# A hybrid decoder block on one core: two output blocks fed in turn, gates and compression inputs reordered, one norm factor and one load moved to ScalarE

## The chip, the cores and the metric

The kernel runs on 1 core of one Trainium2 chip. The metric is the device time of one execution in microseconds (us), as the median of several runs. Five engines work side by side, each through its own queue in program order: PE (TensorE, matrix products into PSUM), DVE (VectorE), ACT (ScalarE), POOL (GpSimd) and SP (SyncE, which here only issues DMA transfers). They wait for one another through semaphores. The profile's PEld is PE's loading of the stationary operand, which overlaps its products.

## What is computed

One decoder block over 512 tokens and a model width of 2048, all in fp32:

```python
hn   = rmsnorm(x, norm1_g)
proj = hn @ w_in                      # q_a k_a v_a | q_b | k_c v_c | k_s v_s | k_w v_w | g_b
# mixer A, 8 heads: windows (128,1) (512,4) (2048,16) of (window, dilation), mixed by their
# softmax denominators, ALiBi slopes
o_a  = dilated_mixture(q_a, k_a, v_a)
# mixer B, 8 heads in 2 key/value groups: keys and values compressed over blocks of 32
# (stride 16) by silu(flat(block + pe) @ w1) @ w2; selected blocks; sliding window
kc, vc = compress_blocks(k_c, ...), compress_blocks(v_c, ...)
g    = sigmoid(g_b)                   # three gates for each head and token
o_b  = g0 * compressed(q_b, kc, vc) + g1 * selected(q_b, k_s, v_s) + g2 * window(q_b, k_w, v_w)
h    = x + concat(rmsnorm(o_a, grp_norm_a), rmsnorm(o_b, grp_norm_b)) @ w_out
hn2  = rmsnorm(h, norm2_g)
h    = h + (silu(hn2 @ w_gate) * (hn2 @ w_up)) @ w_down      # hidden width 5632
out  = rmsnorm(h, final_g)
```

## The kernel before

**Layout and precision.** Features lie on the 128 partitions, the 512 tokens on the free axis. Every fp32 product is made of three products in a reduced format: an operand X is split into a high part h (ACT, a copy that rounds) and a low part l (DVE, X minus h), and PE adds `wh*ah + wh*al + wl*ah` (`mm3`, lines 164 to 167; `mm`, lines 1009 to 1012). `ah` and `al` hold the split activations, 16 blocks of 128 features each.

**The weight stream.** `plan()` lists the units of weights (128 x 1024) in the order in which they are used; SP loads them four ahead into `raw` (`load_to`, line 102). Each unit is two *halves* of 128 x 512, and each half is a `Job`: `first()` is the ACT copy to `wh` (line 136), `second()` the DVE subtraction to `wl` (line 139). `wh` and `wl` have five buffers, so a half's copy can start once PE has used up the half five before it. `next_half()` (line 172) hands PE the next half; at that place in the program the `first()` of the half three further on is emitted and the `second()` of the half two further on, then what `later(n, f)` has put off by n halves. `run_unit` (line 193) runs the products of a list, four blocks of 128 x 128 to a half, and calls `side_hook` after every second block: in it, the small tasks of a stage are slipped between PE's products.

**The stages.**

1. Input blocks (lines 278 to 308): SP loads `sm` (all small constants and gains, 64 KB), then the blocks `xc` of x and the weights. `split_act` (line 252) multiplies a block by its gain from `sm` while it splits it into `ah`, `al`. PE makes the four compression inputs `pc` (k_c and v_c of two groups) as the blocks arrive, then the 24 gate columns `pg` (lines 315 to 317). The factor 1/rms is made for tokens by `Rsqrt`, and `Spread` (line 230) turns it into a full 128 x 512 tile: four 128 x 128 diagonal matrices (identity times a column, line 237, DVE), then four products with ones (line 243). The result is `r1`.
2. Shared keys and values of group 0 (`kv_group`, line 658): the projections ks, kw, vs, vw, two half-units each of 24 products. Meanwhile eight `kv_part` tasks (line 330), one for each side hook, scale `pc` by `r1` into `kv_src` (line 333, DVE, for every second task), add the position embedding in another order of elements (line 341, DVE: it reads `kv_src` with a step of 16 elements and writes `ku` in sequence), and split the result (line 343, ACT; line 328, DVE). After the first half-unit of ks, `gates_out` scales `pg` (line 360, DVE), transposes it on PE (line 363) and makes the gates. The first layer of the compression, 16 units `w1` (line 370) of eight short products (256 columns), is laid between the projections as `W1_AFTER` says: for each name, how many units follow its two half-units. The w1 units use the `kv_part` results; after unit 7 and unit 15 ACT copies the sums to `hids` (line 386), and `compressed(s)` (line 388) does the rest in two steps.
3. Heads (lines 694 to 726): for each of 8 j, projections qb, qa, ka, va, with attention in the side hook: `step()` (line 581) alternates between scores (`s_steps`) and transposes with the product by values (`t_steps`, the last of them `pv`). A `pv` step waits at least `SLACK` = 2 steps after the last transposes. In the last head, after the first half of va, `split_act` for the eight blocks of mixer B (into `ah[0..7]`) is put off over the next four halves, two blocks to a half.
4. Output projection (lines 886 to 896): 16 blocks of 128 features over the B half, then 16 over the A half. Each block (`out_unit`, line 830) has a PSUM bank (tag `proj` for blocks 0 and 1; there are two `proj` banks, and the last va projection has used one of them, which `evac_v`, line 441, reads out on DVE), two halves of weights, and needs `ah[0..3]` in its first half, `ah[4..7]` in its second. `last_steps` finishes the attention here; when it is idle, `close_attention` splits the A blocks, makes the group norms and loads x again.
5. FFN: for each of 44 blocks f of hidden features, seven products P1 to P7 of 256 columns (a Strassen-like scheme; `product`, line 997), then combinations on DVE (`after`, line 1027); a down projection after each four f. For f = 0 the norm factors are made on the way (lines 1089 to 1097): two `Spread`s, `inv` and `r2`. P1's PSUM bank is read at line 1047 before f = 1 can start in it.
6. The last down projection and the final norm (`last`, line 1104).

## Time and profile before

| | |
|---|---|
| median of 3 runs | 2183.11 us (2182.37 to 2186.63) |
| the profiled execution's own time | 2182.41 us |
| its span, first to last instruction | 2180.6 us |
| PE busy | 2161.7 us (99%), 15776 products |
| DVE busy | 1568.4 us (72%) |
| ACT busy | 970.5 us (45%) |
| granted TensorE clock | 0.998 |
| moved by DMA | 232.28 MB, mean 107 GB/s |

The profile page gives busy time by engine, the chain of work that ended last, and groups of instructions by source line. The lists of waits name, for each engine, the instruction that waited and what it waited for. The timeline gives every instruction with its start and length; PE's products are pipelined, so that the pace of PE is read from start to start (a product of 512 columns takes a row of about 0.39 us, while the next starts about 0.23 us after it). What stands in square brackets at the end of a timeline row is the time the engine sat idle before it, and what released it. Two instructions of one kind that follow each other are merged in one row, with their count behind an x.

### The profile page before, as it was taken

The page shows a single profiled execution, that of the slowest core. Times are in us where ns is not written, and L with a number is a line of the kernel's source. Part 1 is how long each engine was busy: PE and PEld are TensorE (multiplying, and loading weights), DVE is VectorE, ACT ScalarE, POOL GpSimd, SP SyncE. Part 2 cuts the span into 40 slices and gives each one's busy share as a digit, 9 for nine tenths or more (in the row PEclk, how much of TensorE's full clock was granted, in tenths as well). Part 3 has the DMA queues.
Part 4 walks back from the last instruction along what each step waited for, and adds up shares of the span by engine and source line. Part 5 has one row for each costly group of instructions (what it writes and reads, how often), then busy time and mean ns, then how long its engine had stood idle before and what let it go on. Part 6 is the DMA issues. An engine that isn't in the chain of part 4 may idle for free.

```text
span 2180.6 us, 39719 instructions
## 1 busy us (share of the span) xinstructions
PE 2161.7 (99%) x15776; PEld 2021.7 (93%) x15776; DVE 1568.4 (72%) x3046; ACT 970.5 (45%) x1862; POOL 43.7 (2%) x51
## 2 busy tenths in 40 slices
PE   9999999999999999999999999999999999999997
PEld 7788888888887889999999999999999999999997
DVE  6755666356667578979687786869596877868686
ACT  6544444244444255535344443535353444435356
POOL 0000000000000000000000000000000000000003
PEclk9999999999999999999999999999999999999999
DMA  6442222322134334343333333333333333333233
GB/s 223 145 138 80 80 81 68 99 90 80 58 100 154 97 97 107 117 117 93 107 112 108 96 117 102 112 88 117 117 98 107 108 112 93 117 107 108 80 125 107
DMA packets 81866, 232.28 MB, mean 107 GB/s; under 512 B 8848, under 2 KB 11536, under 8 KB 81680
## 3 DMA queue, kind: packets, MB, share of 16 engines
q1 hardware_dynamic: 80960, 228.17, 33.2%
q0 software_dynamic: 720, 1.57, 0.5%
q8 instruction: 124, 2.03, 0.4%
q14 instruction: 62, 0.51, 0.1%
HBM read 225.51 MB, written 4.19 MB: 105 GB/s over the span
## 4 chain that ended last, share of the span: by engine, by line
PE 96%; DVE 2%; ACT 1%; issue 0%; DMA 0%; SPq 0%; DVEq 0%; ACTq 0%
PE P L1012 15%; PE P L1010 15%; PE P L1011 15%; PE pp L165 6%; PE pp L167 6%; PE pp L166 6%; PE pd L1011 4%; PE pd L1010 4%; PE pd L1012 4%; PE pab L166 3%; PE pab L167 3%; PE pab L165 3%; PE pt L515 1%; PE psc L167 1%; PE psc L166 1%; PE psc L165 1%
## 5 line engine op out<-in xcount | busy, mean ns | idle before, releaser
L136 ACT ACTIVATE wh<-raw 128x512 fp32r<-128x512 f32 x888 | 549.2, 628 | 533.5 <-PE P L1011 209.6
L139 DVE TENSOR_TENSOR wl<-raw,wh 128x512 fp32r<-128x512 f32 x888 | 596.5, 685 | 47.4 <-ACT wh L136 46.9
L1012 PE MATMUL P<-ah,wl 128*128 128x256 f32 x1552 | 428.9, 276 | 0.3 <-DVE wl L139 0.3
L1010 PE MATMUL P<-ah,wh 128*128 128x256 f32 x1552 | 428.8, 276 | 0.0
L1011 PE MATMUL P<-al,wh 128*128 128x256 f32 x1552 | 428.8, 276 | 0.0
L1012 PEld LDWEIGHTS P<-ah,wl 128*128 128x128 f32 x1552 | 291.4, 188 | 0.5 <-DVE wl L139 0.5
L1011 PEld LDWEIGHTS P<-al,wh 128*128 128x128 f32 x1552 | 291.4, 188 | 0.0
L1010 PEld LDWEIGHTS P<-ah,wh 128*128 128x128 f32 x1552 | 291.4, 188 | 0.0
L165 PE MATMUL pp<-ah,wh 128*128 128x512 f32 x640 | 260.5, 407 | 0.0
L167 PE MATMUL pp<-ah,wl 128*128 128x512 f32 x640 | 251.0, 392 | 0.0
L166 PE MATMUL pp<-al,wh 128*128 128x512 f32 x640 | 250.3, 391 | 0.0
L754 DVE TENSOR_TENSOR raw<-raw 128x512 f32<-128x512 f32 x346 | 237.3, 686 | 3.4
L1010 PE MATMUL pd<-ah,wh 128*128 128x256 f32 x784 | 216.6, 276 | 0.0
L1012 PE MATMUL pd<-ah,wl 128*128 128x256 f32 x784 | 216.6, 276 | 0.0
L1011 PE MATMUL pd<-al,wh 128*128 128x256 f32 x784 | 216.5, 276 | 0.0
L136 ACT ACTIVATE wh<-rawd 128x512 fp32r<-128x512 f32 x160 | 101.2, 632 | 247.8 <-PE pd L1011 123.5
L1078 DVE TENSOR_TENSOR hs<-hs,pd 128x512 f32<-128x512 f32 x98 | 67.4, 688 | 122.9 <-PE pd L1012 122.7
L1011 PEld LDWEIGHTS pd<-al,wh 128*128 128x128 f32 x784 | 147.2, 188 | 0.0
L1010 PEld LDWEIGHTS pd<-ah,wh 128*128 128x128 f32 x784 | 147.2, 188 | 0.0
L1012 PEld LDWEIGHTS pd<-ah,wl 128*128 128x128 f32 x784 | 147.2, 188 | 0.0
L167 PEld LDWEIGHTS pp<-ah,wl 128*128 128x128 f32 x640 | 120.2, 188 | 27.9
L139 DVE TENSOR_TENSOR wl<-rawd,wh 128x512 fp32r<-128x512 f32 x160 | 110.1, 688 | 40.7 <-ACT wh L136 35.6
(275 smaller groups left out, 4565.4 us busy)
## 6 DMA issues: line engine op xcount, KB each, us to landing
raw<-in_wst_dram SPq DMA_DIRECT2D x310, 512.0 KB, 3.5
rawd<-in_wdn_dram SPq DMA_DIRECT2D x160, 256.0 KB, 2.6
bias<-in_bias_dram SPq DMA_DIRECT2D x16, 320.0 KB, 3.0
xc<-in_xt_dram SPq DMA_DIRECT2D x16, 256.0 KB, 3.3
hs<-in_xt_dram SPq DMA_DIRECT2D x16, 256.0 KB, 5.0
fin<-in_wdn_dram SPq DMA_DIRECT2D x8, 512.0 KB, 3.9
out_dram<-hs SPq DMA_DIRECT2D x8, 256.0 KB, 2.1
out_dram<-scaled SPq DMA_DIRECT2D x3, 512.0 KB, 2.8
```

What stands on the lines that cost most here:

```text
L136: act.activation(self.h, self.src(), AF.Copy)
L139: dve.tensor_tensor(self.l, self.src(), self.h.bitcast(F32), op=OP.subtract)
L165: pe.matmul(o, wh, mh, start=start, stop=False)
L166: pe.matmul(o, wh, ml, start=False, stop=False)
L167: pe.matmul(o, wl, mh, start=False, stop=stop)
L515: pe.transpose(p[:, 128 * (o + b):128 * (o + b) + 128], self.e[t][:, 128 * b:128 * b + 128], ident)
L754: return lambda: dve.tensor_tensor(o(), o(), x(), op=OP.add)
L1010: pe.matmul(o, wh, mh, start=start, stop=False, skip_group_check=True)
L1011: pe.matmul(o, wh, ml, start=False, stop=False, skip_group_check=True)
L1012: pe.matmul(o, wl, mh, start=False, stop=stop, skip_group_check=True)
L1078: dve.tensor_tensor(hs[:, nb, :], hs[:, nb, :], p, op=OP.add)
```

## The change

- `W1_AFTER`: after the change the 16 w1 units follow the projections in groups of 3 (after kw's second half-unit), 4 and 3 (vs), 3 and 3 (vw); before, in groups of 3 and 3 (kw), 3 and 3 (vs), 2 and 2 (vw).
- Output projection: the weight halves of blocks 0 and 1 are used in turn (block 0 first half, block 1 first half, block 0 second half, block 1 second half), and both `proj` banks are taken at the start.
- `Spread` can make its diagonals on ACT; the factor `inv` before the FFN does so.
- `sm` is loaded by a DMA that ACT issues and not SP.
- `kv_part`: the scaling writes `kv_src` in the element order that the addition reads, with a step of 32 elements; the addition reads it in sequence.
- The scaling of `pg` becomes a task of its own, third in the list of tasks, ahead of the third `kv_part`.
- `step()`: for the last head, the `pv` steps wait one step more (`late`).
- In `after` for f = 0 the reading of P1's bank comes one DVE instruction earlier.

```diff
-W1_AFTER = {"ks": (0, 0), "kw": (3, 3), "vs": (3, 3), "vw": (2, 2)}
+W1_AFTER = {"ks": (0, 0), "kw": (0, 3), "vs": (4, 3), "vw": (3, 3)}
...
     n_plain = len(jobs)
+    k = 2 * units.index(("out", 0, 1))
+    jobs[k + 1], jobs[k + 2] = jobs[k + 2], jobs[k + 1]
...
-        def __init__(self, col):
+        def __init__(self, col, on_act=False):
...
             for t in range(self.n):
-                dve.tensor_scalar(self.r[:, 128 * t:128 * t + 128], ident, col[:, t:t + 1], None, op0=OP.mult)
+                r = self.r[:, 128 * t:128 * t + 128]
+                if on_act:
+                    act.activation(r, ident, AF.Copy, scale=col[:, t:t + 1])
+                else:
+                    dve.tensor_scalar(r, ident, col[:, t:t + 1], None, op0=OP.mult)
...
-    sp.dma_start(sm, smalls)
+    act.dma_start(sm, smalls)
...
             kv_src[0] = tmp()
-            dve.tensor_tensor(kv_src[0], pc[2 * s + g], r1, op=OP.mult)
-        tv = kv_src[0].rearrange("p (c i) -> p i c", i=16)
+            dve.tensor_tensor(kv_src[0].rearrange("p (i c) -> p c i", i=16),
+                              pc[2 * s + g].rearrange("p (c i) -> p c i", i=16),
+                              r1.rearrange("p (c i) -> p c i", i=16), op=OP.mult)
+        tv = kv_src[0].rearrange("p (i c) -> p i c", i=16)
...
+    gated = []
+
+    def gates_in():
+        gated.append(tmp())
+        dve.tensor_tensor(gated[0][:48, :], pg[:48, :], r1[:48, :], op=OP.mult)
+
+    tasks.insert(2, gates_in)
+
     def gates_out():
-        t = tmp()
-        dve.tensor_tensor(t[:48, :], pg[:48, :], r1[:48, :], op=OP.mult)
+        t = gated[0]
...
-    cur = {"s": None, "t": None, "ready": deque(), "turn": 0}
+    cur = {"s": None, "t": None, "ready": deque(), "turn": 0, "late": 0}
...
-                    if is_pv and (cur["tat"] + SLACK > now[0] or (a.v is not None and not a.v.ready())):
+                    if is_pv and (cur["tat"] + SLACK + cur["late"] > now[0] or (a.v is not None and not a.v.ready())):
...
             if j == NH - 1 and half == 0:
+                cur["late"] = 1
...
-    for nb in range(KB):
+    first = [ps.tile([128, 512], F32, tag="proj", name="pab", bufs=2) for _ in range(2)]
+    run_unit([(first[n], ah[:, 4 * k + s, :], al[:, 4 * k + s, :], k == 0 and s == 0, k == 1 and s == 3)
+              for k in range(2) for n in range(2) for s in range(4)])
+    pab.extend(enumerate(first))
+    for nb in range(2, KB):
...
         elif name == "P6":
             sub(g[:, HI], g[:, LO], x("P6"))
+            if not f:
+                dve.tensor_tensor(g[:, LO], x("P1"), st["r2"][:, LO], op=OP.mult)
             add(u[:, LO], g[:, HI], x("P7"))
             if not f:
-                dve.tensor_tensor(g[:, LO], x("P1"), st["r2"][:, LO], op=OP.mult)
...
-                later(1, lambda r=r: st.update(inv=Spread(r.z), r2=Spread(r.y)))
+                later(1, lambda r=r: st.update(inv=Spread(r.z, True), r2=Spread(r.y)))
```

## The prediction, written before the result was known

> **What bounds the kernel now.** I read the page first, then the list of PE's waits, then the timeline round each wait.
>
> ```profile
> PE 2161.7 (99%) x15776; PEld 2021.7 (93%) x15776; DVE 1568.4 (72%) x3046; ACT 970.5 (45%) x1862; POOL 43.7 (2%) x51
> PE 96%; DVE 2%; ACT 1%; issue 0%; DMA 0%; SPq 0%; DVEq 0%; ACTq 0%
> ```
>
> PE is busy for 99% of the span and holds 96% of the chain that ended last. The change takes no product away from PE, so all it can win is time in which PE waits. These waits are few, and each has a place:
>
> ```profile
> PE pab L166 <- DVE al L255: 1.6, 2, 0.9
> PE phid L383 <- DVE wl L139: 1.6, 2, 1.1
> PE pgt L363 <- ACT kvs L343: 1.3, 1, 1.3
> PE po L165 <- ACT et_h L523: 0.4, 1, 0.4
> ...
> PE pc L166 <- DVE al L255: 0.3, 1, 0.3
> ```
>
> Columns: us in total, times, longest; the two rows left out, 0.3 each, stand in the FFN's part below. These rows count from the modelled end of the product before. Start to start, a wait costs more: the next product should start 0.23 us after one of 512 columns (64.74 and 64.97 below), 0.12 us after one of 256 (24 of them from 88.82 to 91.55 below), and the first after a wait is slow by another 0.1 us. So I take each loss from starts. All of this makes some 9 us out of 2180: the change cannot win more than about 0.4%.
>
> **The start.**
>
> ```profile
> 0.74 0.38 SPq L278 DMA_DIRECT2D sm<-in_smalls_dram  x1
> 1.18 0.42 SPq L283 DMA_DIRECT2D xc<-in_xt_dram  x1
> sm<-in_smalls_dram SPq DMA_DIRECT2D x1, 64.0 KB, 1.8
> 2.03 0.20 ACT L93 ACTIVATE ident<-ones 128x1 f32<-128x1 f32 x1
> 6.92 0.63 ACT L136 ACTIVATE wh<-raw 128x512 fp32r<-128x512 f32 x1 [1.28 <-DMA raw<-in_wst_dram]
> ```
>
> Without `sm` in front, every load on SP is issued 0.44 us earlier (1.18 - 0.74). ACT's second weight copy waits for its load until 6.92; the next blocks of x follow behind that copy on ACT, and PE's wait for `al` behind them. So the gain is up to 0.44 us, if `sm` is there in time. On ACT it is issued at 0.74 at the earliest, at 2.23 (2.03 + 0.20) at the latest, and took 1.8 us on SP: it lands between 2.5 and 4.0. No row shows a DMA issued by ACT. At the worst I let `sm` land with the slowest load, at 6.92: then the split of x and the first weight copy (0.63 each) come before the second copy, and 1.3 us are lost. I take a gain of 0.35, near the issue rows. A landing up to about 5.6 costs nothing.
>
> [...]
>
> **Gates and compression.**
>
> ```profile
> 64.74 0.39 PE L166 MATMUL pp<-al,wh 128*128 128x512 f32 x1
> 64.97 0.39 PE L167 MATMUL pp<-ah,wl 128*128 128x512 f32 x1
> 66.63 0.42 PE L363 MATMUL pgt<-ident,tmp 48*128 48x48 f32 x4 [1.27 <-ACT kvs L343]
> L341 DVE TENSOR_TENSOR ku<-tmp,sm x8: 1014/1028/1053, 59.4 to 75.1; 128x512 f32<-128x512 f32 x4, 128x496 f32<-128x496 f32 x4
> L333 DVE TENSOR_TENSOR tmp<-pc,r x4: 683/690/701, 58.7 to 72.7; 128x512 f32<-128x512 f32 x4
> 77.99 0.28 PE L382 MATMUL phid<-wh,kvs 128*128 128x256 f32 x1
> 83.23 0.28 PE L383 MATMUL phid<-wl,kvs 128*64 128x256 f32 x1
> 88.82 0.28 PE L382 MATMUL phid<-wh,kvs 128*128 128x256 f32 x1
> 91.55 0.28 PE L383 MATMUL phid<-wl,kvs 128*64 128x256 f32 x1
> 79.79 4.29 DVE L139 TENSOR_TENSOR wl<-raw,wh 128x512 fp32r<-128x512 f32 x7
> 99.25 0.39 ACT L386 ACTIVATE osb<-phid 128x256 f32<-128x256 f32 x1 [0.33 <-PE phid L383]
> 108.75 0.28 PE L382 MATMUL phid<-wh,kvs 128*128 128x256 f32 x1
> 109.11 0.34 PE L383 MATMUL phid<-wl,kvs 128*64 128x256 f32 x1
> ```
>
> The transposes of the gates start at 66.63 and not at 64.97 + 0.23 = 65.20: 1.43 us lost. ACT is named, but the operand `tmp` is DVE's, queued behind four `kv_part` tasks. Third in the list, the scaling has before it one scaling, two additions and one low part. DVE starts these at 58.7; at 1.0, 2 x 0.6 and 0.6 us (prices below), plus 0.6 for itself, it is done by 62.2, three us early. Gain 1.4; ends 0 and 1.5 (with the slow restart).
>
> Line 341 takes 1.03 us where line 333, as large, takes 0.69. It reads with a step of 16 elements, that is 64 bytes. After the change eight additions read in sequence, and four scalings write with a step. No row shows a strided write: its ends are 0.69 and, the nearest row with a step, 1.03; I take 1.03. In DVE's queue a plain operation takes 0.61 (4.29 / 7). So DVE saves 8 x 0.4 - 4 x 0.4 = 1.6 us, all of it beside PE.
>
> Three w1 units take PE from 77.99 to 83.23 in the first group and from 88.82 to 91.55 in the second: 5.24 against 2.73, so 2.5 us are lost in the first, where DVE is still behind with the `kv_part` list. After the change this group stands one half-unit (24 products, 5.5 us) later. I add up DVE's queue to see what is late next. After the gates' transposes (65.2 to about 65.6) DVE adds their halves and begins the next `wl` at 66.1. Up to the `wl` of kw's second half-unit then stand one `wl`, four additions, four low parts, two scalings (1.03), another `wl`, ks's scaling and low part with 0.7 between them for ACT, and this `wl` itself: 13 x 0.61 + 2 x 1.03 + 0.7 = 10.7, so 76.8. PE wants it at 65.6 + 2 x 5.46 + 0.45 = 77.0. It is just in time, and the next ones gain on PE.
>
> Inside a group PE uses a half in 0.48 us (2.73 / 6) and DVE makes one in 0.61, but four stand ready; with 0.13 a half this lasts for the eight halves of the group of four. One new stall: unit 7 is now the first of its group, so ACT's copy to `hids` (0.39, after 0.2 for PE's end) stands before the copy of the sixth half of that group, and its `wl` comes at about 2.8 us, where PE wants it at 2.5: with restart and the half after it, 0.45. The stall at 109.11 (0.36 - 0.12 = 0.25), behind ACT's work for the compressed keys in the middle of a group, goes, as that work moves to the end of one. Net: 2.5 + 0.25 - 0.45 = 2.3; ends 0 and 2.8.
>
> **The first output blocks.**
>
> ```profile
> 658.16 0.39 PE L167 MATMUL pab<-ah,wl 128*128 128x512 f32 x1
> 658.93 0.49 PE L165 MATMUL po<-et_h,vwh 128*128 128x512 f32 x1 [0.38 <-ACT et_h L523]
> 661.94 0.68 DVE L443 TENSOR_TENSOR tmp<-pp,r 128x512 f32<-128x512 f32 x1
> 662.20 0.39 PE L167 MATMUL pab<-ah,wl 128*128 128x512 f32 x1
> 662.69 0.49 PE L165 MATMUL pab<-ah,wh 128*128 128x512 f32 x1
> 663.94 0.50 PE L166 MATMUL pab<-al,wh 128*128 128x512 f32 x1 [0.75 <-DVE al L255]
> 665.56 0.47 PE L165 MATMUL pab<-ah,wh 128*128 128x512 f32 x1
> 666.89 0.50 PE L166 MATMUL pab<-al,wh 128*128 128x512 f32 x1 [0.86 <-DVE al L255]
> ```
>
> Lost now: 0.54 before `po` (658.93 - 658.16 - 0.23) and 0.2 in its slow start; 0.26, 1.02 and 0.1 round 663; 1.10 and 0.1 at 666.9. Together 3.3. With the halves in turn, `ah[4..7]` are wanted 5 us later, past all four waits for `ah` and `al`; with one step more, `po` follows twelve products and not six, and its operands are ready.
>
> What is late next: block 1 is started after 12 products and `po`. Counted on from 658.16 + 0.23 = 658.39, six products (1.39) and `po` (1.92 without waits) end at 661.70. Block 1's bank is the one the last va projection used, and DVE reads that out only at 661.94 to 662.62, behind a chain of softmax steps that does not depend on PE there. So PE waits until 662.68 and restarts slowly: 1.1. Behind this wait PE's queue holds the transposes of the last head. Net 2.2; ends 0 (`po` and the bank wait as bad as what goes) and 3.3. The later `pv` steps also put off the closing of the attention, with its sixteen loads of x, by one half: all work of the closing, SP's loads among it, moves together, and PE has no listed wait between 667 and 866 to make worse. The bank of block 0 is wanted four blocks (22 us) later; the cover is wide.
>
> **FFN start.**
>
> ```profile
> 859.60 1.65 DVE L237 TENSOR_SCALAR r<-ident,rs 128x128 f32<-128x128 f32 x8
> 863.54 0.60 ACT L246 ACTIVATE r<-prb 128x512 f32<-128x512 f32 x1 [1.92 <-PE prb L243]
> 866.06 0.28 PE L1012 MATMUL P<-ah,wl 128*128 128x256 f32 x1
> 866.63 0.39 PE L1010 MATMUL P<-B11h,wh 128*128 128x256 f32 x1 [0.29 <-DVE ft L1047]
> 875.08 0.28 PE L1011 MATMUL P<-al,wh 128*128 128x256 f32 x1
> 875.64 0.39 PE L1012 MATMUL P<-ah,wl 128*128 128x256 f32 x1 [0.29 <-DVE wl L139]
> ```
>
> Half of the eight diagonals leave DVE: 0.83 us less. Four on ACT cost between that and four of L246's 0.60, so 0.8 to 2.4; ACT sits idle for 1.92 just after, which hides what I take (1.1); without that cover they would delay the copy of `r2`. DVE soon waits for ACT's next `wh`, which itself follows that copy, so most of the 0.83 is lost to waiting. Line 1047 comes one instruction earlier, some 0.4: the first stall (0.45 + 0.1) goes to about 0.1. The second (0.44 + 0.1) stands at the end of a DVE queue that moves up less than PE does, and grows by a little. Net 0.3; ends 0 and 1.1.
>
> **Sum.** 0.35 + 1.4 + 2.3 + 2.2 + 0.3 = 6.55. The profiled execution took 2182.41 (span 2180.6, 1.8 around it), 0.7 under the median of 2183.11. It gives 2175.9 from the profiled time, 2176.6 from the median: I say 2176.2. By the upper ends (0.44 + 1.5 + 2.8 + 3.3 + 1.1 = 9.1) it is 2173.3.
>
> **Rivals.**
>
> - *The broadcast operand of line 341, not its step, makes it slow.* Then it stays at 1.03 and the four scalings rise: the queue above grows by four additions x 0.42, to 78.5 where PE wants 77.0: 1.6 us come back, with the next half. Time 2177.8. Both rows fit it. Chance 0.1. [...]
> - *The output blocks win nothing*: the bank wait and the later closing take all 2.2. Time 2178.4. For it speaks that DVE and ACT alternate in that softmax chain; against it, that the lost 3.3 are four separate waits for work that is then long done. Chance 0.15.
> - *`sm` is late on ACT's queue*, up to 6.92: 1.65 worse than my term, 2177.9. Chance 0.1.
> - *The edit of the order doesn't do what it says*: w1's wait follows it, since DVE has no rest from 58.7 to 84; with half of the 2.3 it is 2177.4. Chance 0.1.
> - *Slower*: a strided write costs far more than a strided read. All four scalings lie ahead of the `wl` that has only 0.2 to spare, and 1.4 more lie in DVE's wait for the gates' transposes. From (6.55 + 1.6) / 4 + 1.03 = 3.1 us for one, the whole gain is gone; from 4.2 it is slower by over 0.2%, say 2188. The one strided row speaks against it. Chance 0.05.
>
> **Chances and range.** The forecast has 0.5. 0.2% is 4.4 us, about what a measurement of this kernel can tell from no change, so 2178.7 is the bound of faster. The forecast and each of the first four rivals alone lie under it, but with two together, or with the spread of the runs (they reach 4.3 over the lowest), the time lies over it: 0.2 for the same, 0.05 for slower, 0.75 for faster. The range goes from the upper ends to two rivals together: 2173.3 to 2180.8. It leaves out the last rival and some of the spread.
>
> **What would show it.** PE's list has no more waits for `kvs` at line 363, for `wl` at the first three w1 units, or for `al` at line 166 near 663; it gains one of about 0.8 us for `pab` on the last `tmp` of line 443, and one at the seventh w1 unit. Line 333 is at 1.03, line 341 at 0.69. The first `wh` waits of ACT end 0.4 earlier. PE's busy time stays. The prediction is wrong if line 341 stays at 1.03, if the group of four w1 units waits, if ACT's first split waits for `sm`, or if new waits stand between 667 and 866.

## The result, and the profile after

| | before | after |
|---|---|---|
| median, us | 2183.18 (2182.37 to 2187.25, 6 runs) | 2176.69 (2175.99 to 2179.86, 6 runs) |
| the profiled execution, us | 2182.41 | 2175.99 |
| its span, us | 2180.6 | 2174.2 |

The ratio is 0.9967, with a 95% interval from 0.9954 to 0.998: faster by 0.33%. The upper end of the interval just touches the 0.2% that the prediction took as the bound of faster. The forecast was 2176.2.

First the page of the kernel after, its busy times and the shares of the chain that ended last:

```profile
PE 2159.6 (99%) x15776; PEld 2022.0 (93%) x15776; DVE 1566.8 (72%) x3042; ACT 971.0 (45%) x1866; POOL 43.7 (2%) x51
PE 98%; DVE 1%; ACT 0%; issue 0%; DVEq 0%; ACTq 0%
```

As many products as before, and PE's share of the chain rises from 96% to 98%: what went is waiting. PE's idle time falls from 18.9 to 14.6 us. Its busy time falls too, by 2.1, where the prediction had it stay: a row of 0.39 runs 0.16 past the moment at which the next product should start (0.23 after its own start), so the first part of a wait counts as busy, and so does the longer row behind it (0.50 at 658.14 below). The list of PE's waits (columns: us in total, times, longest) is now

```profile
PE prb L249 <- DVE r L243: 1.7, 1, 1.7
PE warm L96 <- DVE ones L92: 1.1, 1, 1.1
PE pab L167 <- DVE tmp L458: 0.9, 1, 0.9
PE pcmp L427 <- DVE et_h L431: 0.7, 1, 0.7
PE P L1032 <- DVE wl L139: 0.7, 1, 0.7
PE prs L213 <- ACT sqt L1150: 0.5, 1, 0.5
PE phid L398 <- DVE wl L139: 0.2, 1, 0.2
```

The lines are those of the kernel after: L167 to L169 were L165 to L167, L249 was L243, L397 and L398 were L382 and L383, L458 was L443, L1030 to L1032 were L1010 to L1012. Gone are the waits for `al` near 663 and 666, for the gates, for `et_h` before `po`, and 1.6 for `wl` at the first w1 units. Three waits are new or longer: `pab` on the last `tmp` of the va projection, `P` on a `wl`, `phid` on a `wl`. The other four rows stood in the list before with the same sizes; the change does not touch them.

For the time by stage I take the start of the same product in both timelines. "Lead" is by how much it comes earlier than in the kernel before:

| product | before, us | after, us | lead | gained in the stage | forecast |
|---|---|---|---|---|---|
| first of the ks projection | 59.75 | 58.59 | 1.17 | 1.17 (start) | 0.35 |
| transposes of the gates | 66.63 | 64.23 | 2.39 | 1.22 (gates) | 1.4 |
| first scores of the heads | 140.93 | 136.36 | 4.57 | 2.18 (w1, compression) | 2.3 |
| first of the FFN | 843.71 | 836.93 | 6.78 | 2.21 (output blocks) | 2.2 |
| first of f=2 | 886.40 | 880.00 | 6.41 | -0.37 (FFN start) | 0.3 |
| end of the span | 2180.64 | 2174.21 | 6.43 | 0.02 | 0 |

The sum, 6.43, is close to the 6.55 forecast. But two terms missed and made up for each other: the start won 0.8 more, the FFN lost where it was to win. That the total came out so close is in part luck. These two terms are the ones the runs go after.

The new places in the timeline of PE after (columns: start, length, engine, line, instruction; in brackets the idle time before and its releaser):

```profile
63.92 0.39 PE L169 MATMUL pp<-ah,wl 128*128 128x512 f32 x1
64.23 0.45 PE L378 MATMUL pgt<-ident,tmp 48*128 48x48 f32 x4
...
101.30 0.28 PE L397 MATMUL phid<-wh,kvs 128*128 128x256 f32 x1
101.76 0.33 PE L398 MATMUL phid<-wl,kvs 128*64 128x256 f32 x1 [0.18 <-DVE wl L139]
...
657.01 0.28 PE L169 MATMUL po<-et_h,vwl 128*128 128x256 f32 x1
658.14 0.50 PE L167 MATMUL pab<-ah,wh 128*128 128x512 f32 x1 [0.86 <-DVE tmp L458]
...
867.88 0.28 PE L1031 MATMUL P<-al,wh 128*128 128x256 f32 x1
868.82 0.39 PE L1032 MATMUL P<-ah,wl 128*128 128x256 f32 x1 [0.67 <-DVE wl L139]
```

The transposes now follow the product before by 0.31, with no wait listed. At 101.76 stands the second half of unit 9 (the units counted from 0), that is the sixth half of the group that unit 7 begins: 0.46 - 0.12 = 0.34 late. This is the place that the prediction works out; its list of signs calls it "the seventh w1 unit". At 658.14 stands block 1, which waits for its bank: 1.13 - 0.12 = 1.01, the 0.9 of the list and the slow restart. At 868.82 one of f=1's last halves is 0.83 late.

The groups of DVE's three lines that were reordered, after (ns min/median/max, first and last start in us):

```profile
L339 DVE TENSOR_TENSOR tmp<-pc,r x4: 1092/1104/1110, 57.4 to 71.1; 128x512 f32<-128x512 f32 x4
L349 DVE TENSOR_TENSOR ku<-tmp,sm x8: 668/681/693, 58.6 to 76.0; 128x512 f32<-128x512 f32 x4, 128x496 f32<-128x496 f32 x4
L370 DVE TENSOR_TENSOR tmp<-pg,r x1: 676/676/676, 60.6 to 60.6; 48x512 f32<-48x512 f32 x1
```

The addition (L349, before L341) falls from 1.03 to 0.68. The scaling (L339, before L333) rises from 0.69 to 1.10. `pg` is scaled by 60.6 + 0.7 = 61.3, three us before PE wants it.

And the start, on SP, ACT and their queues, after:

```profile
1.04 0.42 ACTq L284 DMA_DIRECT2D sm<-in_smalls_dram  x1
3.78 0.72 ACT L260 ACTIVATE ah<-xc,sm 128x512 fp32r<-128x512 f32 x1 [1.55 <-DMA sm<-in_smalls_dram]
4.41 0.61 ACT L136 ACTIVATE wh<-raw 128x512 fp32r<-128x512 f32 x1
5.58 0.63 ACT L136 ACTIVATE wh<-raw 128x512 fp32r<-128x512 f32 x1 [0.57 <-DMA raw<-in_wst_dram]
```

ACT issues `sm` at 1.04, its first split waits for it until 3.78, and still starts 0.30 before the 4.08 of the kernel before. The second weight copy, 6.92 before, is at 5.58: 1.34 earlier, with its load issued only 0.47 earlier (1.65, not 2.12).

### The profile page after: what moved, and what is told of

It reads as the page before. It is cut to its first block, busy times and chain, and to the rows that moved or that the text cites. A ratio compares the mean times of both kernels' runs of the same rounds, so it can differ in the third digit from the quotient of the medians.

```text
span 2174.2 us, 39722 instructions
## 1 busy us (share of the span) xinstructions
PE 2159.6 (99%) x15776; PEld 2022.0 (93%) x15776; DVE 1566.8 (72%) x3042; ACT 971.0 (45%) x1866; POOL 43.7 (2%) x51
## 3 DMA queue, kind: packets, MB, share of 16 engines
q0 software_dynamic: 720, 1.57, 0.5%
## 4 chain that ended last, share of the span: by engine, by line
PE 98%; DVE 1%; ACT 0%; issue 0%; DVEq 0%; ACTq 0%
PE P L1032 15%; PE P L1031 15%; PE P L1030 15%; PE pp L167 7%; PE pp L169 7%; PE pp L168 7%; PE pd L1031 4%; PE pd L1032 4%; PE pd L1030 4%; PE pab L167 3%; PE pab L169 3%; PE pab L168 3%; PE pt L530 1%; PE psc L169 1%; PE psc L168 1%; PE psc L167 1%
## 5 line engine op out<-in xcount | busy, mean ns | idle before, releaser
L1032 PE MATMUL P<-ah,wl 128*128 128x256 f32 x1552 | 428.9, 276 | 0.7 <-DVE wl L139 0.7
L1030 PE MATMUL P<-ah,wh 128*128 128x256 f32 x1552 | 428.8, 276 | 0.0
L1032 PEld LDWEIGHTS P<-ah,wl 128*128 128x128 f32 x1552 | 291.4, 188 | 0.9 <-DVE wl L139 0.9
L1030 PEld LDWEIGHTS P<-ah,wh 128*128 128x128 f32 x1552 | 291.4, 188 | 0.0
L167 PE MATMUL pp<-ah,wh 128*128 128x512 f32 x640 | 260.6, 407 | 0.0
L169 PE MATMUL pp<-ah,wl 128*128 128x512 f32 x640 | 251.0, 392 | 0.0
L1032 PE MATMUL pd<-ah,wl 128*128 128x256 f32 x784 | 216.5, 276 | 0.0
L1030 PE MATMUL pd<-ah,wh 128*128 128x256 f32 x784 | 216.5, 276 | 0.0
L1030 PEld LDWEIGHTS pd<-ah,wh 128*128 128x128 f32 x784 | 147.2, 188 | 0.0
L1032 PEld LDWEIGHTS pd<-ah,wl 128*128 128x128 f32 x784 | 147.2, 188 | 0.0
L169 PEld LDWEIGHTS pp<-ah,wl 128*128 128x128 f32 x640 | 120.2, 188 | 28.3 <-DVE wl L139 0.4
```

What stands on the lines that cost most here:

```text
L167: pe.matmul(o, wh, mh, start=start, stop=False)
L169: pe.matmul(o, wl, mh, start=False, stop=stop)
L1030: pe.matmul(o, wh, mh, start=start, stop=False, skip_group_check=True)
L1032: pe.matmul(o, wl, mh, start=False, stop=stop, skip_group_check=True)
```

## The experiments

My theory after the comparison: the start's gain is the issue time and what the landing of the second weight half adds by chance; the FFN's loss comes from a DVE chain that did not move with PE. The rivals: that taking `sm` out of SP's queue alone gives the whole gain of the start; that the FFN's edits themselves lose; that one of the other edits (`late`, the strided scaling, `W1_AFTER`) carries more or less than its term. Kernels marked "from before" change the kernel before; all others change the kernel after. Leads are against the one profile of the kernel before, as in the table above:

| kernel | ks | gates | scores | FFN | f=2 | end | time, us |
|---|---|---|---|---|---|---|---|
| after | 1.17 | 2.39 | 4.57 | 6.78 | 6.41 | 6.43 | 2175.99 |
| b_sm (from before) | 0.72 | 0.72 | 0.69 | 0.79 | 0.76 | 0.25 | 2182.16 |
| b_smlate (from before) | -0.54 | -0.56 | -0.58 | -0.58 | -0.61 | -0.61 | 2183.01 |
| a_kv | 0.93 | 2.27 | 3.69 | 5.89 | 5.52 | 1.56 | 2180.86 |
| a_w1 | 1.08 | 2.27 | 0.55 | 2.77 | 2.39 | -1.99 | 2184.43 |
| a_w1b | 0.59 | 1.77 | 1.08 | 3.30 | 2.92 | 2.42 | 2179.99 |
| a_w1e | 0.46 | 1.65 | 0.94 | 3.11 | 2.73 | 2.16 | 2180.26 |
| a_bank | 0.92 | 2.11 | 4.28 | 7.70 | 7.32 | 7.34 | 2175.09 |
| a_late0 | 0.39 | 1.58 | 3.74 | 5.98 | 5.60 | 5.62 | 2176.80 |
| a_invdve | 0.57 | 1.76 | 3.94 | 6.20 | 5.65 | 5.67 | 2176.74 |
| a_early | 0.38 | 1.58 | 3.74 | 6.03 | 6.31 | 5.82 | 2176.62 |
| a_ffn | 0.38 | 1.57 | 3.71 | 5.96 | 5.52 | 1.12 | 2181.29 |
| c_all | 0.61 | 1.80 | 4.36 | 7.74 | 8.42 | 7.93 | 2174.49 |

The time is that of the profiled execution.

### The start alone: b_sm and b_smlate

b_sm, from before, makes only the move of the load:

```diff
-    sp.dma_start(sm, smalls)
+    act.dma_start(sm, smalls)
```

> The kernel before with one edit: the load of sm issued by ACT. Theory A (the prediction's term): every load on SP moves up by the 0.44 us of one issue, so the second half of the first weights lands at about 6.5 and the first product on the third block of x starts at about 12.1, against 12.53 before. Theory B: the small transfer at the head of SP's queue held the loads behind it back by more than its issue; then the half lands at about 5.6 and that product starts at about 11.2, as in the changed kernel. Either way the rest of the run is as before, and the span is shorter by 0.4 (A) or 1.2 to 1.3 us (B).

2182.16 where the kernel before took 2182.13 on the same chip. Two rows of ACT's timeline in b_sm:

```profile
3.86 0.72 ACT L254 ACTIVATE ah<-xc,sm 128x512 fp32r<-128x512 f32 x1 [1.62 <-DMA sm<-in_smalls_dram]
...
6.16 0.63 ACT L136 ACTIVATE wh<-raw 128x512 fp32r<-128x512 f32 x1 [0.83 <-DMA raw<-in_wst_dram]
```

The first split waits for `sm` much as in the kernel after, but the second weight half lands 0.58 later (6.16, not 5.58), with the same issue times. That is between the two theories (about 6.5 and 5.6). Over the twelve profiles here in which ACT loads `sm`, this copy starts between 5.58 and 6.42, the lead at ks runs from 0.38 to 1.17 and is 0.68 on average; the profiled execution of the kernel after has the largest. So the size of the gain in one execution is in good part chance. The mean would make the edit worth 0.7, but all leads have one profile of the kernel before as their base, and its landing is one draw from such a spread as well: 6.92 less the 0.47 of the issue is 6.45, at the upper edge of the twelve. How much of the 0.68 lies beyond the issue time is not shown. In b_sm most of the lead is lost at the very end, in four products that are told of below.

b_smlate, from before, leaves `sm` on SP but behind the first block of x and the first weights:

```diff
-    sp.dma_start(sm, smalls)
     load_x(0)
     load_to(1)
+    sp.dma_start(sm, smalls)
     load_x(1)
```

> The kernel before with the load of sm left on SP, but issued behind the first block of x and the first weights. If it is the place at the head of the queue that costs (B), the second half of the first weights lands at 5.6 here too, sm (issued at about 2.1) at 4 to 4.7, and the first product on the third block of x starts at 11.2 to 11.6. If it takes a queue of its own on ACT, this kernel gains at most the 0.4 us of the issue: 12.1 or later.

2183.01. The row of ACT's first split in b_smlate:

```profile
5.75 0.72 ACT L254 ACTIVATE ah<-xc,sm 128x512 fp32r<-128x512 f32 x1 [3.51 <-DMA sm<-in_smalls_dram]
```

Issued at 2.12 among other loads, `sm` takes 3.5 us to land, not 1.8 (before) or 2.6 (after), and the start loses 0.54. Neither expectation came about: `sm`, which was to land at 4 to 4.7, lands at 5.7 and is now what the first split waits for. So getting `sm` out of the way of x and weights is not enough: it must still be issued early, and the issue by ACT does both. On the rival this run says one thing more. The second weight half's load takes 3.7 us from issue to landing here and lands at 5.3, as theory B has it; it takes 4.8 in the kernel before, and 3.9 to 4.7 in the twelve profiles. So theory B, that the small load at the head of SP's queue costs more than its issue, stays open; against single profiles of the two kernels it is not shown either.

### The order of the compression inputs: a_kv

The kernel after, with the scaling in sequence and the addition with a step, as before:

```diff
-            dve.tensor_tensor(kv_src[0].rearrange("p (i c) -> p c i", i=16),
-                              pc[2 * s + g].rearrange("p (c i) -> p c i", i=16),
-                              r1.rearrange("p (c i) -> p c i", i=16), op=OP.mult)
-        tv = kv_src[0].rearrange("p (i c) -> p i c", i=16)
+            dve.tensor_tensor(kv_src[0], pc[2 * s + g], r1, op=OP.mult)
+        tv = kv_src[0].rearrange("p (c i) -> p i c", i=16)
```

> The changed kernel with the compression inputs in their old order: line 341 at 1.03 us again, the scaling at 0.69. By the queue that the prediction adds up, the low part of kw's second half-unit then comes 4 x 0.42 - 2 x 0.34 = 1.0 us later, with 0.2 to spare in the sum: PE waits there for 0.7 to 1.0 us, and the first attention score starts that much after 136.36. Rival 1: the order is hidden anyway, no wait, same time within 0.2. Rival 2: it costs all the 1.6 us that DVE has more to do.

Between gates and scores it gains 1.42 (3.69 - 2.27) where the kernel after gains 2.18. PE's row at the second half-unit of kw, in a_kv:

```profile
76.81 0.50 PE L169 MATMUL pp<-ah,wl 128*128 128x512 f32 x1 [0.46 <-DVE wl L139]
```

This is the place of the prediction's queue sum. DVE's row of that `wl` in a_kv is

```profile
76.07 0.68 DVE L139 TENSOR_TENSOR wl<-raw,wh 128x512 fp32r<-128x512 f32 x1
```

and in the kernel after

```profile
75.45 0.68 DVE L139 TENSOR_TENSOR wl<-raw,wh 128x512 fp32r<-128x512 f32 x1
```

Without the reordering it comes 0.6 later, while PE is only 0.1 behind (leads of 2.27 and 2.39). So the reordering is worth 0.76. The time of 2180.86 says more than that: another 4 us go between f=2 (lead 5.52) and the end (1.56). They have nothing to do with this edit, and are told of under the pace.

### The order of the w1 units: a_w1 and a_w1b

The kernel after with the old order:

```diff
-W1_AFTER = {"ks": (0, 0), "kw": (0, 3), "vs": (4, 3), "vw": (3, 3)}
+W1_AFTER = {"ks": (0, 0), "kw": (3, 3), "vs": (3, 3), "vw": (2, 2)}
```

> The changed kernel with the w1 units where they were (3 and 3 after kw, 3 and 3 after vs, 2 and 2 after vw). By the prediction's queue, DVE is 1.6 us lighter and the gates 1.2 us earlier, for DVE as well as for PE, so the first group still comes before DVE has caught up: a loss of 1.5 to 2.5 us at its three units, 0.25 later for the compressed keys, and no wait at the seventh unit. The first attention score starts 1.2 to 2.4 us after 136.36. Rival: the lighter tasks alone have done it, then it starts within 0.3 of 136.36 and the move of the units is worth nothing.

The lead of 2.27 at the gates falls to 0.55 at the scores, a loss of 1.72. PE's row at the first w1 units, in a_w1:

```profile
78.94 0.36 PE L398 MATMUL phid<-wl,kvs 128*64 128x256 f32 x1 [1.95 <-DVE wl L139]
```

DVE's queue sets when this `wl` is ready, and PE only comes there earlier and waits longer. But the wait is not all of the 1.72, as the second profile of this kernel shows.

The same kernel again, for its spread:

> The kernel with the old W1_AFTER once more, for its spread over several executions. If the long slow stretch of the 256-column products belongs to this kernel, all its executions are near 2184.4; if it falls on some executions whatever the kernel, most are near 2180.4 (the starts up to f=2 were 2.4 us ahead of the kernel before, whose time is 2182.6) and a few near 2184.4.

a_w1b has the same wait (1.96), yet between gates and scores it loses only 0.69 (1.77 to 1.08), and a_w1e below, with the same order, 0.71. The stretch behind the wait in a_w1, and then in a_w1b (columns: stretch, length, PE busy and its instructions, granted clock, DMA share, GB/s):

```profile
78.90:82.50 3.60, 3.56 (x17) 0.53 0.62 206
78.90:82.50 3.60, 3.06 (x20) 1.00 0.54 164
```

In a_w1 the granted clock falls to about half behind the wait, and PE starts a product of 256 columns each 0.21 us and not each 0.12. That costs the other 1.03. It came in one of three profiles with this wait. With the other edits in place the new order is therefore worth 2.18 + 0.7 = 2.9, where 1.2 to 2.4 was expected, and more in an execution in which the clock falls. Without it, 0.7 of the gates' 1.2 is lost again. The prediction's terms added up since all edits were made at once; one by one they do not add.

The ten runs of a_w1b: median 2183.95, ratio 1.0003 (0.9993 to 1.0012). They fall into two groups: 2179.99, 2180.18, 2180.27, 2180.57, and 2183.40, 2184.51, 2184.73, 2184.77, 2184.82, 2185.10. The means, 2180.25 and 2184.56, are 4.3 apart. So the 4 us come and go with the execution, but on this kernel more often than not, while one of the 21 runs of the kernel before beside it lies up there (2187.24).

### The output blocks: a_bank and a_late0

a_bank gives block 1 another bank than the one the va projection leaves late, and block 3 the other `proj` bank:

```diff
-    first = [ps.tile([128, 512], F32, tag="proj", name="pab", bufs=2) for _ in range(2)]
+    first = [ps.tile([128, 512], F32, tag=t, name="pab", bufs=2) for t in ("proj", "sc")]
...
-        p = out_unit(1, ("proj", "sc", "t")[nb // 2 % 3])
+        p = out_unit(1, "proj" if nb == 3 else ("proj", "sc", "t")[nb // 2 % 3])
```

> The changed kernel with another PSUM bank for output block 1: one of the score banks, read out long before, and block 3 takes the bank of the last va projection in its stead. The prediction's reading (the new wait is for the DVE read of the va bank): PE's wait for tmp of line 458, 0.9 us, goes, no other wait of over 0.3 us comes, and the first FFN product starts 0.8 to 1.1 us earlier than 836.93. Rival: the split of blocks 6 and 7 of ah is then late, as before the change, and takes 0.5 us or more of it back.

The first waits in PE's list of a_bank:

```profile
PE prb L249 <- DVE r L243: 1.7, 1, 1.7
PE warm L96 <- DVE ones L92: 1.1, 1, 1.1
PE pcmp L427 <- DVE et_h L431: 0.7, 1, 0.7
PE P L1032 <- DVE wl L139: 0.6, 1, 0.6
```

The wait for `tmp` is gone and no other takes its place. From scores to FFN it gains 3.42, against 2.21 in the kernel after: 1.2 more, the prediction's 1.1 for the bank and the whole 3.3 of the old waits.

a_late0 leaves out the extra step:

```diff
-                cur["late"] = 1
```

> The changed kernel without the extra step before the last head's products by values. If each wait removed is its own gain (as the prediction has it, 0.54 and 0.2), the product po waits for et_h again and the first FFN product starts 0.5 to 0.7 us after 836.93. Rival: block 1 waits for its PSUM bank until the same moment in any case, so the old wait only takes time out of the new one: same start within 0.2.

From scores to FFN it gains 2.24: the same. PE's list of a_late0 has, in place of the wait for `tmp`,

```profile
PE po L167 <- ACT et_h L538: 0.4, 1, 0.4
```

So the rival came about. Without the extra step `po` stands ahead of its operands; with it, PE comes to block 1 that much earlier and waits for the bank. As long as the bank is not free, the edit of `step()` is worth nothing.

### The FFN's start: a_invdve, a_ffn and a_early

a_invdve writes the diagonals of `inv` on DVE again:

```diff
-                later(1, lambda r=r: st.update(inv=Spread(r.z, True), r2=Spread(r.y)))
+                later(1, lambda r=r: st.update(inv=Spread(r.z), r2=Spread(r.y)))
```

> The changed kernel with the four diagonals of inv on DVE again. If the relief of DVE (0.83 us) was lost in its wait for ACT's next weight copy (0.63 in the changed kernel), PE's start of f = 1 and of f = 2 stay within 0.25 us of 859.45 and 880.00. Rival 1: ACT's 1.27 us for these four made the copies late, and without it f = 2 starts 0.3 us or more earlier. Rival 2: DVE's queue carries it all, f = 2 starts 0.6 to 0.8 later.

From the first product of the FFN to f=2 it loses 0.55 (6.20 to 5.65), the kernel after 0.37: the diagonals on ACT are worth at most 0.2, by one run of each kernel.

a_ffn undoes both edits, this one and the place of P1's product with `r2`:

> The changed kernel without both edits at the FFN's start (VectorE writes both factors' diagonals, and P1's product with r2 stands behind the add of P7). The changed kernel lost 0.37 us between the first product of the FFN and the start of f=2, against the kernel before. If the edits themselves lose it, this kernel loses nothing there (within 0.1). If the edits gain as forecast (0.3) and the loss is VectorE's chain, which did not move as far as TensorE, it loses 0.6 to 0.9, and the wait on the wl at 868 us is 1.0 us or more.

It loses 0.44 up to f=2, more than the first expectation allows and less than the second. The two rows of its list for this stretch are

```profile
PE P L1032 <- DVE wl L139: 0.3, 1, 0.3
PE P L1030 <- DVE ft L1067: 0.3, 1, 0.3
```

These are the two waits of the kernel before, unchanged. The kernel after has lost the one on `ft` (its lead grows from 6.78 to 7.18 over f=0, while a_ffn's stays at 5.96 and 5.95) and has the other at 0.7. So a_ffn's 0.44 is no wait: it comes behind the wait at 869, where PE's products start every 118 ns and not every 113 (the pace, below). The kernel after has this pace as well, from 868 to 880, and there it costs 0.42 (868.82 to 880.00 is 11.18 long, 875.64 to 886.40 before 10.76). The edit of P1 does win at the first stall (0.4; 0.33 in a_invdve, which has this edit alone), and the second stall gives it back. Why is plain in DVE's timeline of the kernel after:

```profile
857.91 0.69 DVE L139 TENSOR_TENSOR wl<-raw,wh 128x512 fp32r<-128x512 f32 x1 [0.63 <-ACT wh L136]
...
861.48 0.69 DVE L139 TENSOR_TENSOR wl<-raw,wh 128x512 fp32r<-128x512 f32 x1
...
868.08 0.69 DVE L139 TENSOR_TENSOR wl<-raw,wh 128x512 fp32r<-128x512 f32 x1
```

and, for the last two, in the kernel before:

```profile
868.21 0.68 DVE L139 TENSOR_TENSOR wl<-raw,wh 128x512 fp32r<-128x512 f32 x1
...
874.90 0.68 DVE L139 TENSOR_TENSOR wl<-raw,wh 128x512 fp32r<-128x512 f32 x1
```

The chain from 861.48 to the late `wl` at 868.08 is 6.60 long; before, it ran from 868.21 to 874.90, 6.69. It moved by 6.73 to 6.82, as much as the FFN's first product (6.78). The 0.83 us less of diagonals did not move it: DVE waited 0.63 for ACT's `wh` instead. PE came by 7.18 earlier, and waits for the difference.

a_early splits one more half ahead of the copy of `r2`, so that this `wh` is there:

```diff
+                split_to(pos["half"] + 3)
                 st["r2"] = st["r2"](tag="t", bufs=2)
```

> The changed kernel with ACT's next weight copy emitted ahead of the copy of r2, which waits for PE. Theory: DVE's wait of 0.63 for that copy goes, all of its queue up to the late wl of f = 1 moves up by that, and PE's wait there falls from 0.83 (by starts) to 0.2 or 0.3. If the slower pace of PE behind that wait (118 ns a product of 256 columns and not 113, until f = 2) is set off by the wait, it goes too: f = 2 starts 0.9 to 1.1 us before 880.00. If the pace has another cause, 0.5 to 0.6 before it. Rival: another wait takes its place, f = 2 within 0.2.

The wait at 868 is no longer in PE's list, and from FFN to f=2 it gains 0.28 where the kernel after loses 0.37: 0.65, near the 0.5 to 0.6 expected for a pace with another cause. The pace is not set off by this wait: in a_early PE has no listed wait in f=1, and its products still start every 118 ns, from the first of the FFN to f=2. By that PE also comes 0.2 later to the place of the old wait (8.63 us after the start of f=1, not 8.44), so the 0.8 that went is DVE's 0.63 and these 0.2.

a_early's time, 2176.62, hides the gain: its start had 0.8 less lead, and it lost 0.5 at the end, in four products. The chain of work that ended last has there, in the kernel after,

```profile
2164.62 0.70 PE prb L249 x4
```

and in a_early

```profile
2164.71 1.21 PE prb L249 x4
```

These are the broadcasts of the last norm, after PE has waited 1.7. They take 1.21 in seven of the profiles here and 0.70 to 0.77 in the seven others, whatever was changed. The granted clock tells the two apart; the kernel after and then a_early over these four products:

```profile
2164.60:2165.30 0.70, 0.68 (x4) 0.98 0.00 0
2164.70:2165.90 1.20, 1.19 (x4) 0.50 0.00 0
```

It is 0.50 in all seven with 1.21, and 0.81 to 1.00 in the others.

### The pace of the 256-column products: a_w1e

a_kv, a_w1 and a_ffn lost some 4 us after f=2, where no edit of theirs acts and where PE has no listed wait. The stretches of time of the kernel after (columns: stretch, length, PE busy and its instructions, granted clock, DMA share, GB/s) and then those of a_kv:

```profile
940.00:980.00 40.00, 40.00 (x355) 1.00 0.35 105
1000.00:1040.00 40.00, 40.00 (x355) 1.00 0.35 106
```

```profile
940.00:980.00 40.00, 40.00 (x342) 1.00 0.36 113
1000.00:1040.00 40.00, 40.00 (x356) 1.00 0.37 119
```

In the same 40 us a_kv gets through 342 products, not 355: one starts each 117 ns and not each 113, at the same granted clock and nearly the same DMA share. In a_kv this slower pace lasts from 869 to 986, in a_w1 from 872 to 989, in a_ffn from 869 to 986. It begins behind the wait for the `wl` near 868 to 872. Up to f=2 the kernel after has the same pace behind this wait; from there to f=5 (881 to 986 in a_kv) it costs them 3.9 us, 0.7 of it in the one block f=2. In the kernel after and in a_bank, a_late0, a_invdve, a_early and a_w1b it ends at 879 to 883. Both ends (880 is the start of f=2, and P1 of f=5 starts at 981 in the kernel after) fall where a block's first half of weights is put into its buffer at the other of two offsets, 64 bytes apart (blocks f=1, f=2 and each eighth from f=5 on).

The slower pace is no work of the change. All 14 profiles have it in f=0, the kernel before's too; there, in f=0 and then in f=2:

```profile
844.00:854.00 10.00, 10.00 (x87) 1.00 0.45 88
888.00:898.00 10.00, 10.00 (x91) 1.00 0.26 79
```

That is 87 products against 91 in 10 us (both counts take in some that run over an edge); from start to start it is 118 ns against 113. In twelve of the profiles it ends with the first half of f=1, which is one of those at the other offset. But such a half does not always end it: a_early and c_all (below) run through that of f=1 at the slower pace, and a_kv, a_w1 and a_ffn through that of f=2. In c_all it ends at 867, at a half that lies at the ordinary offset.

a_w1e adds one such block to a_w1:

```diff
-        r["P1", 0].even = f in (1, 2) or f % 8 == 5
+        r["P1", 0].even = f in (1, 2, 3) or f % 8 == 5
```

> The changed kernel with the old W1_AFTER, and f=3 among the blocks whose first half-unit takes the other offset. Theory that the slow pace of the 256-column products (118 ns for 113) ends where a half-unit takes the other offset: a slow stretch that begins at about 872 us ends at the start of f=3, near 907 us, not at 989, and the profiled execution is some 3.4 us below the one with f=5 (82 us at 5 ns for each 118 ns), 2181.0. Rival, that the stretch belongs to the execution and its end has nothing to do with the offset: it ends at 989 again or at no such place, 2184.4 where it occurs. If the stretch does not occur at all in this execution, the profile tells nothing on its end, and the runs' spread against the same kernel without the edit is what is left.

Its profiled execution did not have the stretch, so the profile does not tell where it ends. The ten runs do: 2180.11 to 2180.46 for four, 2181.14 to 2182.05 for six; median 2181.18, ratio 0.9993 (0.9984 to 1.0002). The upper group is 1.2 above the lower, not 4.3, and nothing is left near 2184.5. One block more at the other offset takes 3.1 off the upper group; an end at f=3 and not at f=5 would take off 3.9 - 0.7 = 3.2. So the theory fits the times, but no profile here shows the end at f=3.

### The three losses mended: c_all

a_bank and a_early together, with the w1 units in other groups:

```diff
-W1_AFTER = {"ks": (0, 0), "kw": (0, 3), "vs": (4, 3), "vw": (3, 3)}
+W1_AFTER = {"ks": (0, 0), "kw": (0, 3), "vs": (3, 3), "vw": (4, 3)}
...
-                        if n1 in (10, 12):
+                        if n1 in (9, 12):
```

> The three losses that the runs so far left in the changed kernel, mended together: block 1 in a bank of the scores (-1.1 us, as measured alone), the split of two more half-units ahead of the r2 copy at the FFN's start (-0.65 by the start of f=2 against the output blocks' end), and W1 set as kw (0,3), vs (3,3), vw (4,3) with a compression step at 9 in place of 10 (-0.2 to -0.4, the stall of the seventh unit). If the losses are independent: 2174.6 us against 2176.7 of the changed kernel, between 2173.9 and 2175.6, none of the three waits left on TensorE. If what one gains is only waited for at the next place (the chain of VectorE at 861 to 868 us does not move with TensorE), the wait at the start of f=1's last halves comes back and the time stays at 2175.1 to 2176.

2174.55 (2174.45 to 2174.99, 5 runs) against 2182.75 of the kernel before on that chip, ratio 0.9964 (0.9952 to 0.9977). Its slowest run is under the fastest of the kernel after, by 1.0; the two were timed on different chips, with the kernel before at 2182.75 and 2183.18, and the ratios' intervals overlap. The stages below show the gain more surely than the totals. PE's whole list of waits in c_all:

```profile
PE prb L249 <- DVE r L243: 1.7, 1, 1.7
PE warm L96 <- DVE ones L92: 1.1, 1, 1.1
PE pcmp L427 <- DVE et_h L431: 0.7, 1, 0.7
PE prs L213 <- ACT sqt L1151: 0.5, 1, 0.5
```

The three waits that were new or longer after are gone, and nothing took their place: gates to scores gains 2.56 (after 2.18), scores to FFN 3.38 (2.21), FFN to f=2 0.68 (-0.37). It is the best version of this study.

## Why the prediction was right, point by point

- **What bounds the kernel**: right. What was won is time in which PE waited, with the slow product behind each wait (a row of 0.50 and not 0.39 at 658.14); the list of PE's waits and the starts in the timeline gave each term its place. The prediction's list of waits leaves out four rows more than it says (`prb`, `warm`, `pcmp`, `prs`: 1.7, 1.1, 0.7, 0.5). None of its terms rests on them, and they are still there after.
- **The start, 0.35**: the loads did move up, but the execution that was compared won 1.17; the mean over the twelve profiles is 0.68. The step that failed is the gain "up to 0.44 us" as an upper end: it took the landing of the second weight load as moved with its issue, and the copy that waits for this landing moved by 0.50 (a_ffn) to 1.34 (after). In nine of the twelve profiles the lead at ks is above 0.44. With one profile of the kernel before as the base, and landings that spread by 0.84 at the same issue times, this does not settle whether the place in the queue costs more than the issue. That the first split would not wait for `sm` was named as a sign, and it does wait, until 3.78; as it begins 0.30 earlier than before all the same, that sign was badly chosen.
- **Gates, 1.4**: 1.22, right. But a_w1b and a_w1e show that with the old order of the w1 units 0.7 of this gain is lost again, which the prediction did not say.
- **Compression, 2.3**: 2.18, right, and by its own steps. The strided write took 1.10 where I took 1.03 from the strided read, and the addition fell to 0.68. DVE saves 8 x 0.347 - 4 x 0.414 = 1.1, not 1.6. The `wl` of kw's second half-unit was to be just in time, and PE's list shows no wait there; a_kv shows it 0.46 late without the reordering, so the margin was read rightly. The stall in unit 9 is 0.34, not 0.45.
- **Output blocks, 2.2**: 2.21, right. The new wait for the bank stands where it was forecast, at 1.01 for 1.1; a_bank takes it away and finds the whole 3.4. `late` itself brought nothing while that wait stands.
- **FFN, 0.3**: wrong in sign, -0.37. The first stall went as forecast and gave 0.40. The step that failed is that the second stall "grows by a little": it grew from 0.44 to 0.83, since DVE won nothing of the 0.83 us (the prediction let most of it be lost to waiting for ACT, it was all). So the two stalls cancel. What is left of the -0.37 is the slower pace from 868 to 880, 0.42, which a_ffn without these edits has as well; the prediction has no term for it. Against a_ffn, the two edits together win 0.07.
- **Rivals**: none came about. The addition did get faster; the blocks did win; `sm` was not late; w1's wait did not follow. The slower case fell with the 1.10 of the strided write.
- **The spread**: the forecast for the median lay 0.5 under it, and the run at 2179.86 was within the range. The range's upper end, 2180.8, is more than two rivals make: the two dearest give 2176.2 + 2.2 + 1.65 = 2180.05.

Not settled is what starts the slower pace, and what lets it run past f=2 in one execution and not in the next. That the runs of the kernel before at 2186.63 and 2187.25, and that of the kernel after at 2179.86, are such executions is likely by their size (3 to 4.5 above the others), but no profile of one was taken.

## What to carry to other kernels

Where PE is busy for 99%, add up what each wait costs by starts, and for each that is taken away ask which queue the next product depends on: the gain stands only if that queue moves as well. Here 0.7 of the gates' 1.2 us needed the new w1 order, and DVE's 0.83 us at the FFN were worth nothing, since DVE then waited for ACT. A wait that a change brings in at a known place, such as a PSUM bank read out late, is worth the next edit: here another bank gave 1.2 us. And judge an edit of under 1 us by the stage in which it acts, and by more than one profile: the totals of single executions differ by more than that for reasons elsewhere (the two groups of a_w1b's runs by 4.3), and one profile of a stage can have the clock fall in it, as a_w1's had (0.53, where a_w1b's had 1.00). So look at the granted clock of the stage before a loss is put down to an edit.

## What the hardware showed that I had not expected

- The 256-column products of the FFN run at one of two paces, about 113 or 117 to 118 ns from start to start, at a granted clock of 1.00. A stretch at the slower pace from f=2 to f=5 costs 3.9 us. Going by the times, it fell on six of ten executions of one kernel (a_w1b), and on one of 21 and two of six of the kernel before. Most of its ends fall on a half of weights that lies at another offset, 64 bytes away (in twelve of 14 profiles the stretch in f=0 ends with such a half, the first of f=1), though not each such half ends it (a_early and c_all run through that of f=1), and with one more such half the slower group of ten runs lay 3.1 lower.
- Behind the same wait the granted clock fell in some executions and not in others. Four products after a wait of 1.7 us took 0.70 at a granted clock of 0.98 (after) and 1.21 at 0.50 (a_early). After a wait of 1.95 us in a_w1 the products of 256 columns started every 0.21 us for the next 3.4 us, at 0.53 over the stretch; after 1.96 in a_w1b it stayed at 1.00.
- With the same issue times, the copy that waits for the second load of weights started between 5.58 and 6.42 in twelve profiles, and a load of 64 KB took 1.8 us at the head of SP's queue, 2.6 from ACT, and 3.5 in the middle of SP's loads.
